# Operand addresses, residual loads and early sums in a three-layer transformer kernel on one core

## The chip, the core and the metric

The kernel runs on one core of a Trainium2 chip (trn2). The metric is the time of the whole program on the device, in microseconds; the median of three runs is compared. All data are float32; matrix products run on pairs of "fp32r" tiles: each operand is split into a high part, which ScalarE writes (`hi`), and the remainder, which VectorE writes (`lo`), and a product is three matmuls, high by high, high by low and low by high.

## The reference

Three residual layers over 1,024 rows of 1,024 columns, then a feed-forward block:

```python
# layer 0: h = rms_norm(x); proj = h @ w_in (18 feature tiles of 128)
#   sliding-window attention (8 heads) * silu(gate), pooling * silu(gate), @ w_out, rms_norm, + x
# layer 1: h = rms_norm(x); a, b, gate = h @ w_in (24 tiles)
#   depthwise causal convolution, 31 taps, of a * sigmoid(b); layer norm; silu * silu(gate); @ w_out ...
# layer 2: 16 meta rows ahead of x; proj = rms_norm(h) @ w_in (24 tiles)
#   attention with decay over all earlier rows, short convolution, head norms, @ w_out, + h
hn = rms_norm_2(h, norm_mlp_g[layer])
a = jnp.square(jax.nn.relu(jnp.einsum('bld,df->blf', hn, w_ff1[layer])))   # 1024 -> 4096
h = h + jnp.einsum('blf,fd->bld', a, w_ff2[layer])                         # 4096 -> 1024
h = rms_norm_2(h, final_norm_g)
return h[:, N_META:]
```

## The kernel before

**Products.** `project_chunk` (line 394) makes one feature tile of 128 for one chunk of rows: 8 steps of 128 inputs times 3 matmuls, 24 products, into a bank of tag `pj`. In layers 0 and 1 there are two chunks of 512 columns (`c0`, `c1`), in layer 2 three of 400, 256 and 384. The stationary operand is a weight tile; `weights` (line 375) loads it into tag `wf` of the pool `stream` and splits it into `wh` and `wl` of the same pool, two buffers each. `out_project` (line 479) makes the three out-projections, with the split rows `yh`, `yl` as stationary and the weights `wo` as moving operand, 48 products of 512 columns a row tile.

**Memory.** SBUF is filled from both ends by pools. From below: 16,384 bytes a partition that the program keeps for dynamic DMA, four constants of 32 bytes, the pool `const` (768 bytes), `stream` (six tiles of 4,096), `small` (2,432), then the pools of the stages; from above the pool `edge` and the stages' "right" pools. Tiles are rounded to 32 bytes. A pool opened over a closed one waits, tile by tile, for the last readers of what lay there.

**Order.** A planner sets the order of each engine's queue by priority (the order of the code) and its own estimate of when an instruction is ready; on the chip every queue runs in that order. All loads and stores but the gates' go through SP's queue.

**Out-projection of layer 2 and the step to the feed-forward.** `mix_ff` (line 1488) runs over eight row tiles: load `x2`, 48 products, add (`finish`, line 1536), store to `x3`, mean square, scale (`scaled`). Both feed-forward matrices are multiplied by a scheme of seven block products instead of eight (Winograd's form of Strassen's). Its right-hand operands are seven blocks of the normed rows, transposed: `b11`, `b21`, `b22` are put in the loop; `t1` to `t4` are sums of rows `i` and `i + 4`, made in `sums` (line 1546), and put behind the loop. A put (line 1526) is four transposes into a bank of tag `ps` (two buffers), `hi` on ScalarE, `lo` on VectorE. `xn7`, the scaled last row, and `gpre`, the gain, lie in the stream tag `wl`.

**First matrix.** `Up` (line 174) runs over 16 blocks `q` of the feed-forward's features: `load` (two loads of 512 KB), `top` (splits `a11`, `a12`), `sums` (four sums on GpSimd into two stream tiles `wl`, then the splits `s21`, `s34`, `a22`), and three groups of products: `first` (24), `middle` (36), `last` (24). `pair` (line 185) takes even blocks' tiles from `stream` and odd ones' from the pool `upa`. `first(0)` and `first(1)` stand in `mix_ff` behind the loop, the rest in `rest` (line 293).

**Second matrix.** `feed_down` (line 1617) makes seven steps, each over eight parts `p` of 256 features: load `act` (512 KB, tag `wf`), load or sum the weights (`w`, or the kept `x` and `y`), split both, 24 products into four banks. At each step's end the banks are added to `res`, the residual, which eight loads bring in at step 0, `p` = 1. After steps 5 and 6 `final_norm` (line 1723) squares both halves of a row tile, takes the root, scales and stores.

Of the kernel before, what the change touches and what calls it, by code (L numbers as in the profile page):

```python
# [173 lines left out]
class Up:  # L174
# [6 lines left out]
    def __init__(self, kern, hb, four):  # L181
        self.k, self.nc, self.hb, self.four = kern, kern.nc, hb, four
        self.raws, self.blocks, self.state = {}, {}, {}
# [24 lines left out]
    def sums(self, q):  # L208
        (a11, a12), (a21, a22) = ((t[:, 0:4], t[:, 4:8]) for t in self.raws.pop(q))
# [7 lines left out]
        for tag, names, src in (("s21", ("s2", "s1"), s21), ("s34", ("s3", "s4"), s34), ("a22", ("a22",), a22)):  # L217
            h, l = (self.pool.tile([128, len(names) * 4, 128], F32R, tag=tag + x, name=tag + x) for x in "hl")
# [74 lines left out]
    def rest(self):  # L293
        for q in range(self.N):
            if q > 1:
                self.first(q)
            if q:
                self.last(q - 1)
            if 0 < q < self.N - 1:
                self.load(q + 1)  # L300
                self.top(q + 1)
            self.sums(q)
            self.middle(q)
        self.last(self.N - 1)
        self.k.close(self.g, self.xp)


class Kernel:
    def __init__(self, ctx, tc, a, out):
# [5 lines left out]
        edge.tile([128, 8], F32, name="edge")  # L315
# [185 lines left out]
    def run(self):  # L501
# [3 lines left out]
        self.const.tile([128, 8], F32, name="even")  # L505
# [65 lines left out]
        ong = op[1].tile([128, 16], F32, name="ong")[:, :KD]  # L571
# [21 lines left out]
        hb, up, hp = self.mix_ff(mixed, wo, wp, early[1])  # L593
# [5 lines left out]
    def mix_out(self, layer, y, xsrc, xdst, wsrc, gpost, gpre, eps, cuts, meta, hooks={}, res=None, wo=None, soon=1, wp=None):  # L599
# [26 lines left out]
        if layer == 1:  # L626
            wq = self.pool("wq1", "right")
            wq[1].tile([128, 32], F32, name="pad")
            extra = [self.pool("e1", "right"), wq]
# [198 lines left out]
    def project_first(self, pool, chunks, jobs, holds):  # L828
# [3 lines left out]
        gain = pool.tile([128, 16], F32, name="gain", bufs=1)[:, :KD]  # L832
# [196 lines left out]
    def layer0_pooling(self, chunks, y, ahead):  # L1029
# [3 lines left out]
        psc = pool.tile([128, 16], F32, name="psc", bufs=1)[:, :4]  # L1033
# [452 lines left out]
    def mix_ff(self, y, wo, wp, four):  # L1486
# [11 lines left out]
        up = Up(self, hb, four)  # L1498
        rp = self.pool("res", "right")
# [6 lines left out]
        gpr = self.stream.tile([128, D], F32, tag="wl", name="gpre")  # L1506
# [19 lines left out]
        def put(name, i, src):  # L1526
            bank = self.ps().rearrange("p (k c) -> p k c", k=4)
# [47 lines left out]
        for t in range(1, NT):  # L1575
# [17 lines left out]
        hb.update({n: block(hp1[1], n) for n in names})  # L1593
        own = self.pool("upa")
        up.own = own[1]
        u = scaled(NT - 1, self.stream.tile([128, D], F32, tag="wl", name="xn7"))
# [18 lines left out]
        return hb, up, (own, hp1, hp0)  # L1615

    def feed_down(self, one):
# [71 lines left out]
        )  # L1689
        for n, (name, right, t0, h) in enumerate(steps):  # L1690
# [7 lines left out]
            for p in range(8):  # L1698
# [6 lines left out]
                if n == 0 and p == 1:  # L1705
                    for i in range(NT):
                        nc.sync.dma_start(out=res[:, i, :], in_=self.x3[i * 128:(i + 1) * 128, :])
                if not end:
                    for k in range(2):
                        for i in range(4):  # L1710
                            matmuls(banks[i], i, k, *ops[p], p + k == 0, p == 7 and k == 1, fresh)
            for i in range(4):
# [6 lines left out]
                if n > 4:  # L1719
                    self.final_norm(t0 + i, [res[:, t0 + i, z] for z in HALF], gfin, left[1])  # L1720
        self.close(res_pool, hold, left, xp)

    def final_norm(self, t, parts, gain, pool):
        nc = self.nc
        ms = self.tiny(2, "fms")
        for i, x in enumerate(parts):
            nc.scalar.activation(
                out=self.pj(), in_=x, func=AF.Square, scale=1.0 / 32, accum_out=ms[:, i:i + 1]
            )
        rs = self.tiny(1, "frs")  # L1730
        nc.gpsimd.tensor_tensor(out=rs, in0=ms[:, 0:1], in1=ms[:, 1:2], op=ALU.add)
        self.rsqrt(rs, rs, EPS_B)
# [79 lines left out]
```

## Time and profile before

| | us |
|---|---|
| median of 3 runs | 2005.93 (2004.78 to 2006.83) |
| the profiled execution | 1999.52 |
| its span, first to last instruction | 1997.7 |

| engine | busy us | share of the span |
|---|---|---|
| PE (TensorE) | 1924.1 | 96% |
| PEld (its weight loads) | 1619.3 | 81% |
| DVE (VectorE) | 1346.7 | 67% |
| ACT (ScalarE) | 907.5 | 45% |
| POOL (GpSimd) | 543.6 | 27% |

The stages, in us from the start: layer 0 to about 376, layer 1 to 777, layer 2's attention to 1,240, its out-projection to 1,339, the first feed-forward matrix to 1,668, the second to 1,990. The profile is one execution; its time stands beside the median for that reason. "PEclk" is the granted TensorE clock as a share of full speed. The chain of waits follows the work that ended last back from the end, at each step to what released it; pieces of one kind are merged. In lists in order of time, brackets give the engine's idle time before an instruction and what ended it. Matmuls are pipelined: one lasts some 390 ns while the next starts after some 230, so the pace is read from a piece of the chain, its length over its count.

### The profile page before, as it was taken

To read this page: it belongs to the slowest core of one execution; us is meant where nothing else is said; L and a number is where in the kernel's file an instruction comes from. 1 tells how busy PE (TensorE), PEld (TensorE's weight loads), DVE (VectorE), ACT (ScalarE), POOL (GpSimd) and SP (SyncE) were. 2 spreads that over 40 slices of the span, in tenths; PEclk is the share of its full clock that TensorE was granted. 3 is DMA by queue.
4 is the path that set the end of the run, shared out by engine and by line. 5 is a ranking of instruction groups with operands and counts; after the bars stand their busy time and mean duration, and the time that the engine had idled before them with its cause. 6 is when DMAs were issued, how large, how long until landed. Compare 5 with 4: busy or idle time off the path is not lost.

```text
span 1997.7 us, 25550 instructions
## 1 busy us (share of the span) xinstructions
PE 1924.1 (96%) x9584; PEld 1619.3 (81%) x9584; DVE 1346.7 (67%) x2045; ACT 907.5 (45%) x1577; POOL 543.6 (27%) x433
## 2 busy tenths in 40 slices
PE   7999999899999899899999999998999998899998
PEld 6888778688778678798999998886888886788886
DVE  7888656799887665565656555556767665754656
ACT  5555334455663665554444544224333333333334
POOL 4122602489996221001010101113323220000003
PEclk9999999999999899999999999998999999999999
DMA  4111144111122731111111203422444357622564
GB/s 149 59 38 33 59 136 126 36 44 53 42 69 102 231 107 55 44 44 44 48 48 46 77 22 131 148 106 78 152 161 157 137 175 294 247 98 102 183 215 150
DMA packets 121596, 212.15 MB, mean 106 GB/s; under 512 B 9449, under 2 KB 58985, under 8 KB 121473
## 3 DMA queue, kind: packets, MB, share of 16 engines
q1 hardware_dynamic: 119168, 206.34, 30.6%
q10 hardware_dynamic: 2304, 4.20, 0.6%
q8 instruction: 75, 1.23, 0.3%
q14 instruction: 49, 0.39, 0.1%
HBM read 156.46 MB, written 54.03 MB: 105 GB/s over the span
## 4 chain that ended last, share of the span: by engine, by line
PE 78%; DVE 8%; DMA 4%; POOL 4%; ACT 2%; issue 2%; SPq 0%; DVEq 0%; POOLq 0%; ACTq 0%
PE pj L400 25%; PE pd L485 11%; PE pd L227 9%; PE pd L1679 7%; PE ps L227 4%; POOL side L1129 4%; DVE acc L1135 3%; PE ps L1679 3%; PE pj L1679 3%; PE o L1410 3%; PE pj L227 2%; PE ps L1386 2%; PE pt L1435 2%; DVE wl L361 1%; DMA y<-in_ff 1%
## 5 line engine op out<-in xcount | busy, mean ns | idle before, releaser
L1129 POOL TENSOR_TENSOR side<-side,tap 128x1024 f32<-128x1024 f32 (+1 forms) x99 | 236.1, 2392 | 20.5 <-ACT tap L1128 13.4
L1135 DVE SCALAR_TENSOR_TENSOR acc<-glu,dw,acc 128x1024 f32<-128x1024 f32 (+1 forms) x162 | 193.8, 1238 | 11.5 <-ACT acc L1133 10.3
L400 PE MATMUL pj<-c0h,wl 128*128 128x512 f32 (+1 forms) x496 | 189.3, 382 | 7.0 <-DVE wl L361 7.0
L400 PE MATMUL pj<-c0h,wh 128*128 128x512 f32 (+1 forms) x496 | 190.4, 384 | 2.2 <-ACT gt L1166 2.1
L400 PE MATMUL pj<-c0l,wh 128*128 128x512 f32 (+1 forms) x496 | 189.0, 381 | 0.0
L400 PE MATMUL pj<-c1h,wh 128*128 128x512 f32 (+1 forms) x496 | 176.7, 357 | 3.3 <-ACT c1h L357 1.6
L400 PE MATMUL pj<-c1h,wl 128*128 128x512 f32 (+1 forms) x496 | 176.8, 356 | 0.0
L400 PE MATMUL pj<-c1l,wh 128*128 128x512 f32 (+1 forms) x496 | 176.7, 356 | 0.0
L1128 ACT ACTIVATE tap<-glu,dw 128x1024 f32<-128x1024 f32 (+1 forms) x99 | 103.7, 1054 | 78.1 <-POOL side L1129 77.5
L357 ACT ACTIVATE ah<-act 128x1024 fp32r<-128x1024 f32 x56 | 59.3, 1061 | 160.8 <-PE ps L1679 74.4
L361 DVE TENSOR_TENSOR al<-act,ah 128x1024 fp32r<-128x1024 f32 x56 | 68.2, 1223 | 91.5 <-ACT ah L357 91.5
L357 ACT ACTIVATE ph<-pt 128x512 fp32r<-128x512 f32 (+3 forms) x144 | 72.5, 516 | 101.1 <-PE pt L1435 66.4
L361 DVE TENSOR_TENSOR wl<-wf,wh 128x1024 fp32r<-128x1024 f32 (+1 forms) x66 | 95.4, 1445 | 25.1 <-ACT wh L357 22.9
L1679 PE MATMUL pd<-bh,ah 128*128 128x512 f32 x256 | 100.3, 397 | 12.4 <-ACT ah L357 12.4
L400 PEld LDWEIGHTS pj<-c0h,wl 128*128 128x128 f32 x496 | 94.4, 190 | 21.6 <-DVE wl L361 7.5
L400 PEld LDWEIGHTS pj<-c1h,wh 128*128 128x128 f32 x496 | 93.4, 188 | 18.7 <-ACT c1h L357 1.8
L400 PEld LDWEIGHTS pj<-c0h,wh 128*128 128x128 f32 x496 | 94.3, 190 | 16.9 <-ACT gt L1166 2.5
L361 DVE TENSOR_TENSOR pl<-pt,ph 128x512 fp32r<-128x512 f32 (+3 forms) x144 | 82.9, 586 | 36.8 <-ACT ph L357 36.2
L400 PEld LDWEIGHTS pj<-c0l,wh 128*128 128x128 f32 x496 | 94.3, 190 | 14.2 <-issue 0.2
L400 PEld LDWEIGHTS pj<-c1l,wh 128*128 128x128 f32 x496 | 93.4, 188 | 14.0 <-DVE c1l L361 0.4
L400 PEld LDWEIGHTS pj<-c1h,wl 128*128 128x128 f32 x496 | 93.5, 188 | 13.3
L1679 PE MATMUL pd<-bl,ah 128*128 128x512 f32 x256 | 100.9, 394 | 0.0
(600 smaller groups left out, 5120.1 us busy)
## 6 DMA issues: line engine op xcount, KB each, us to landing
wf<-in_w SPq DMA_DIRECT2D x63, 512.0 KB, 3.5
raw<-in_ff SPq DMA_DIRECT2D x32, 512.0 KB, 4.9
w<-in_ff SPq DMA_DIRECT2D x32, 512.0 KB, 4.4
act<-acts SPq DMA_DIRECT2D x32, 512.0 KB, 3.2
acts<-s SPq DMA_DIRECT2D x48, 256.0 KB, 3.8
act<-act SPq DMA_DIRECT2D x24, 512.0 KB, 3.8
wf<-in_wo SPq DMA_DIRECT2D x20, 512.0 KB, 3.8
cb<-cum SPq DMA_DIRECT2D x8, 520.0 KB, 4.1
```

Source lines behind the costliest of these rows:

```text
L227: self.nc.tensor.matmul(out=bank, lhsT=st[:, k, :], rhs=mv[:, k, :], start=(start and k == 0 and j == 0), stop=(k == 3 and j == 2), skip_g ...
L357: self.nc.scalar.activation(out=out, in_=src, func=AF.Copy, scale=scale)
L361: return self.nc.vector.tensor_tensor(out=out, in0=src, in1=hi.bitcast(F32), op=ALU.subtract)
L400: self.nc.tensor.matmul(out=p[:m, :n], lhsT=st[:, k, :], rhs=mv[:, k, :], start=(k == 0 and j == 0), stop=(k == KD - 1 and j == 2),)
L485: self.nc.tensor.matmul(out=ops[hf], lhsT=st, rhs=mv[:, HALF[hf]], start=(first and k == ks[0] and j == 0), stop=(last and k == ks[-1] and ...
L1128: nc.scalar.activation(out=tap, in_=src, func=AF.Copy, scale=w)
L1129: nc.gpsimd.tensor_tensor(out=side, in0=side, in1=tap, op=ALU.add)
L1135: nc.vector.scalar_tensor_tensor(out=acc, in0=src, scalar=w, in1=acc, op0=ALU.mult, op1=ALU.add)
L1386: nc.tensor.matmul(out=s[:, :b0 - a0], lhsT=q[e][:, n * 128:(n + 1) * 128], rhs=k[e][j][:, a0:b0], start=(j == 0), stop=(j == 1),)
L1410: nc.tensor.matmul(out=ov[:, cols], lhsT=v[e][:rows, j, :], rhs=mv, start=first, stop=(last and jj == 1),)
L1435: nc.tensor.transpose(pt[:, c:c + 128], ts[i][:, META + 128 * j:META + 128 * (j + 1)], self.ident)
L1679: nc.tensor.matmul(out=bank, lhsT=st[:, k, c], rhs=mv[:, k, :], start=(fresh and first and j == 0), stop=(last and j == 2), skip_group_che ...
```

## The change

1. The program is told to keep 2,048 bytes a partition for dynamic DMA instead of 16,384.
2. `Even`, a wrapper around every pool that `Kernel.pool` opens, rounds tiles up to multiples of 64 elements (256 bytes). Fill tiles are added to or enlarged in `edge`, `const`, `small` and `wq1`.
3. `gpre` moves from `stream` into the pool of `res`, `xn7` into the place of `t4`'s low half. `Up.sums` is cut in two: `add_up` (the GpSimd sums) and `split_sums`. For block 0, `add_up` and the split of `s21` (into a new pool `up21`) are written at the end of the out-projection's loop, the splits of `s34` and `a22` behind the puts. The puts behind the loop are regrouped name by name around `first(0)`, `load(1)`, `top(1)` and `first(1)`; `t2` and `t3` go through banks of tag `pj`.
4. In `feed_down`, `res` is loaded in four quarters of four row tiles by half the columns, each at `p` = 3 of the step that first adds to it.
5. In step 6 the half of each row that is complete is squared, and the epsilon added, ahead of the last products.

```diff
+    def add_up(self, q):
         (a11, a12), (a21, a22) = ((t[:, 0:4], t[:, 4:8]) for t in self.raws.pop(q))
...
+        self.wide[q] = {"s21": (("s2", "s1"), s21), "s34": (("s3", "s4"), s34), "a22": (("a22",), a22)}
+
+    def split_sums(self, q, tags):
+        for tag in tags:
+            names, src = self.wide[q].pop(tag)
+            pool = self.early if tag == "s21" else self.pool
+            h, l = (pool.tile([128, len(names) * 4, 128], F32R, tag=tag + x, name=tag + x) for x in "hl")
             self.split(h, l, src)
...
-            self.sums(q)
+            if q:
+                self.sums(q)
...
+class Even:
+    def tile(self, shape, dtype, **kw):
+        n = int(np.prod(shape[1:]))
+        if n % 64 == 0:
+            return self.pool.tile(shape, dtype, **kw)
+        t = self.pool.tile([shape[0], n + -n % 64], dtype, **kw)[:, :n]
+        return t if len(shape) == 2 else t.rearrange("p (a b) -> p a b", b=shape[2])
...
-        edge.tile([128, 8], F32, name="edge")
+        edge.tile([128, 56], F32, name="edge")
+        self.const.tile([128, 32], F32, name="even")
...
-        return g, g.__enter__()
+        return g, Even(g.__enter__())
...
-        self.const.tile([128, 8], F32, name="even")
+        self.const.tile([128, 8], F32, name="even2")
+        self.small.tile([128, 8], F32, tag="even3", name="even3")
...
+        ep = self.pool("up21", "right")
+        up.early = ep[1]
         rp = self.pool("res", "right")
...
-        gpr = self.stream.tile([128, D], F32, tag="wl", name="gpre")
+        gpr = rp[1].tile([128, D], F32, name="gpre")
...
+        up.add_up(0)
+        up.split_sums(0, ("s21",))
         self.close(tp, wp)
         hp1 = self.pool("h3b")
...
-        for n in names[:2]:
-            for i in range(3):
-                put(n, i, rows[i][n])
-        up.load(1)
-        sums(3, u)
-        for n in names[:2]:
-            put(n, 3, rows[3][n])
+        banks = {"t2": self.pj, "t1": self.ps, "t3": self.pj, "t4": self.ps}
+        def all_puts(n):
+            for i in range(4):
+                put(n, i, rows[i][n], banks[n])
+        sums(3, scaled(NT - 1, xn7[:, 0:2].rearrange("p a b -> p (a b)")))
         self.close(*xp[::-1])
         up.xp = self.psum_pool("pxup", "pd")
         up.first(0)
+        all_puts("t2")
+        up.load(1)
+        all_puts("t1")
         up.top(1)
-        for n in names[2:]:
-            for i in range(4):
-                put(n, i, rows[i][n])
+        all_puts("t3")
         up.first(1)
+        hb["t4"] = block(hp1[1], "t4")
+        all_puts("t4")
         self.close(rp)
         up.g = self.pool("up", "right")
         up.pool = up.g[1]
+        up.split_sums(0, ("s34", "a22"))
...
+        quarters = {0: (0, 0), 1: (4, 1), 2: (0, 1), 4: (4, 0)}
...
-                if n == 0 and p == 1:
-                    for i in range(NT):
-                        nc.sync.dma_start(out=res[:, i, :], in_=self.x3[i * 128:(i + 1) * 128, :])
+                if p == 3 and n in quarters:
+                    r0, c = quarters[n]
+                    for i in range(r0, r0 + 4):
+                        nc.sync.dma_start(out=res[:, i, HALF[c]], in_=self.x3[i * 128:(i + 1) * 128, HALF[c]])
...
+            if n == 6:
+                for i in range(4):
+                    ms = squares[i] = self.tiny(2, "fms")
+                    junk = left[1].tile([128, 512], F32, tag="r", name="junk")
+                    self.half_square(ms, 1, res[:, t0 + i, HALF[1]], junk)
+                    nc.gpsimd.tensor_scalar(
+                        out=ms[:, 1:2], in0=ms[:, 1:2], scalar1=EPS_B, scalar2=None, op0=ALU.add
+                    )
...
-    nc = bacc.Bacc("TRN2", target_bir_lowering=False, num_devices=1)
+    nc = bacc.Bacc("TRN2", target_bir_lowering=False, num_devices=1, dynamic_dma_scratch_size=2048)
```

## Rows read from the trace of the kernel before

**Rows 1.** Busy by stretch: length; PE, PEld, DVE, ACT, POOL; PEclk, DMA share, GB/s

```profile
37.00:260.00 223.00, 220.87 (x1142) 185.65 (x1142) 179.21 (x393) 109.05 (x260) 65.87 (x58) 1.00 0.14 47
...
390.00:570.00 180.00, 170.15 (x722) 136.82 (x722) 170.54 (x152) 106.79 (x112) 163.28 (x69) 0.98 0.14 47
570.00:651.00 81.00, 80.27 (x340) 64.50 (x340) 63.22 (x55) 41.58 (x47) 62.49 (x28) 0.98 0.28 96
...
1339.00:1372.00 33.00, 24.79 (x123) 18.98 (x122) 24.63 (x33) 15.38 (x25) 6.89 (x6) 0.88 0.23 80
...
1667.00:1729.00 62.00, 49.06 (x198) 38.73 (x197) 37.21 (x34) 21.51 (x22) 0.00 (x0) 0.94 0.96 365
```

**Rows 2.** The chain of waits, whole span: start, length, what, merged count

```profile
333.09 28.44 PE pd L485 x124
...
600.53 33.46 PE pj L400 x144
...
777.23 4.37 PE pj L400 x24
...
1435.73 2.77 PE pj L227 x12
...
1454.82 2.72 PE pj L227 x12
...
1772.36 43.52 PE pd L1679 x192
```

**Rows 3.** TensorE in order of time, layer 1's gates: start, length, what, idle before

```profile
570.62 0.50 PE L400 MATMUL pj<-c0h,wh 128*128 128x512 f32 x1 [2.08 <-ACT gt L1166]
```

**Rows 4.** Groups by line and shape, TensorE: count | busy us, mean ns | idle

```profile
L400 PE MATMUL pj<-c0h,wh 128*128 128x400 f32 x184 | 64.6, 351 | 0.0
...
L400 PE MATMUL pj<-c0h,wv 128*128 128x400 f32 x16 | 4.4, 348 | 0.7 <-DVE q L363 0.7
```

**Rows 5.** TensorE in order of time, out-projection to feed-forward

```profile
1338.93 1.03 PE L1529 MATMUL ps<-ident,res 128*128 128x128 f32 x8
...
1360.51 1.96 PE L1529 MATMUL ps<-ident,res 128*128 128x128 f32 x8 [0.81 <-DVE t2l L361]
1363.03 1.11 PE L1529 MATMUL ps<-ident,res 128*128 128x128 f32 x4 [0.56 <-DVE t3l L361]
...
1371.22 0.79 PE L227 MATMUL pd<-t2h,s21h 128*128 128x512 f32 x1 [1.63 <-ACT s21h L357]
```

**Rows 6.** VectorE and GpSimd in order of time, the same stretch

```profile
1342.73 1.29 DVE L1521 SCALAR_TENSOR_TENSOR xn<-res,rs,gpre 128x1024 f32<-128x1024 f32 x1
...
1346.40 2.28 DVE L361 TENSOR_TENSOR a<-raw,a 128x1024 fp32r<-128x1024 f32 x1
...
1355.00 1.28 DVE L361 TENSOR_TENSOR t1l<-ps,t1h 128x512 fp32r<-128x512 f32 x2
...
1365.08 1.27 POOL L216 TENSOR_TENSOR sums<-raw 128x512 f32<-128x512 f32 x1 [17.49 <-PE ps L1529]
```

**Rows 7.** VectorE in order of time, the first reader of `gpre`

```profile
1268.21 1.28 DVE L1521 SCALAR_TENSOR_TENSOR xn<-res,rs,gpre 128x1024 f32<-128x1024 f32 x1 [1.50 <-POOL rs L430]
```

**Rows 8.** SP's queue and TensorE in order of time, start of the second matrix

```profile
1691.77 9.59 SPq L1707 DMA_DIRECT2D res<-x3s  x8
...
1716.84 0.50 PE L1679 MATMUL pd<-bh,ah 128*128 128x512 f32 x1 [3.17 <-ACT ah L357]
```

**Rows 9.** All engines in order of time, the end of the span

```profile
1991.43 0.58 ACT L1727 ACTIVATE pj<-res 128x512 f32<-128x512 f32 x1
...
1992.49 0.22 POOL L427 TENSOR_SCALAR frs<-frs 128x1 f32<-128x1 f32 x1
```

**Rows 10.** DMA queues (packets, MB, share); issues: count, KB, median us to landing

```profile
q1 hardware_dynamic: 119168, 206.34, 30.6%
...
w<-in_ff SPq DMA_DIRECT2D x32, 512.0 KB, 4.4
...
act<-acts SPq DMA_DIRECT2D x32, 512.0 KB, 3.2
```

More of the change, by code (lines that the diff above doesn't have):

```diff
@@ L182, in __init__ @@
         self.k, self.nc, self.hb, self.four = kern, kern.nc, hb, four
-        self.raws, self.blocks, self.state = {}, {}, {}
+        self.raws, self.blocks, self.state, self.wide = {}, {}, {}, {}
     def pair(self, q, tag):
@@ L208, in sums @@
     def sums(self, q):
+        self.add_up(q)
+        self.split_sums(q, ("s21", "s34", "a22"))
+    def add_up(self, q):
         (a11, a12), (a21, a22) = ((t[:, 0:4], t[:, 4:8]) for t in self.raws.pop(q))
@@ L570, in run @@
         wo, stage = {}, {}
-        ong = op[1].tile([128, 16], F32, name="ong")[:, :KD]
+        ong = op[1].tile([128, KD], F32, name="ong")
         nc.sync.dma_start(out=ong, in_=a["ong"])
@@ L592, in run @@
         wp = self.layer2(chunks, last, fs, early, ahead, prefetch)
-        hb, up, hp = self.mix_ff(mixed, wo, wp, early[1])
+        up, hp = self.mix_ff(mixed, wo, wp, early[1])
         up.rest()
@@ L831, in project_first @@
         nc.vector.memset(ones, 1.0)
-        gain = pool.tile([128, 16], F32, name="gain", bufs=1)[:, :KD]
+        gain = pool.tile([128, KD], F32, name="gain", bufs=1)
         ws = [
@@ L1032, in layer0_pooling @@
         pool = pb[1]
-        psc = pool.tile([128, 16], F32, name="psc", bufs=1)[:, :4]
+        psc = pool.tile([128, 4], F32, name="psc", bufs=1)
         nc.sync.dma_start(out=psc, in_=a["psc"])
@@ L1524, in scaled, with put @@
             return out
-        def put(name, i, src):
-            bank = self.ps().rearrange("p (k c) -> p k c", k=4)
+        def put(name, i, src, bank=self.ps):
+            bank = bank().rearrange("p (k c) -> p k c", k=4)
             for k in range(4):
@@ L1592, in mix_ff @@
         names = ("t2", "t1", "t3", "t4")
-        hb.update({n: block(hp1[1], n) for n in names})
+        hb.update({n: block(hp1[1], n) for n in names[:3]})
+        xn7 = hp1[1].tile([128, 4, 512], F32, tag="t4l", name="xn7")
         own = self.pool("upa")
         up.own = own[1]
-        u = scaled(NT - 1, self.stream.tile([128, D], F32, tag="wl", name="xn7"))
-        for n in names[:2]:
-            for i in range(3):
-                put(n, i, rows[i][n])
-        up.load(1)
-        sums(3, u)
-        for n in names[:2]:
-            put(n, 3, rows[3][n])
+        banks = {"t2": self.pj, "t1": self.ps, "t3": self.pj, "t4": self.ps}
[3 more added lines that the diff above has]
+        sums(3, scaled(NT - 1, xn7[:, 0:2].rearrange("p a b -> p (a b)")))
         self.close(*xp[::-1])
@@ L1614, in mix_ff @@
         up.pool = up.g[1]
-        return hb, up, (own, hp1, hp0)
+        up.split_sums(0, ("s34", "a22"))
+        return up, (ep, own, hp1, hp0)
     def feed_down(self, one):
@@ L1719, in feed_down, with half_square, final_norm @@
                 if n > 4:
-                    self.final_norm(t0 + i, [res[:, t0 + i, z] for z in HALF], gfin, left[1])
+                    self.final_norm(t0 + i, [res[:, t0 + i, z] for z in HALF], gfin, left[1], squares.get(i))
         self.close(res_pool, hold, left, xp)
-    def final_norm(self, t, parts, gain, pool):
+    def half_square(self, ms, i, x, junk):
+        self.nc.scalar.activation(out=junk, in_=x, func=AF.Square, scale=1.0 / 32, accum_out=ms[:, i:i + 1])
+    def final_norm(self, t, parts, gain, pool, ms=None):
         nc = self.nc
[L1725 to L1729, printed above, removed]
+        before = ms is not None
+        if not before:
+            ms = self.tiny(2, "fms")
+            self.half_square(ms, 1, parts[1], self.pj())
+        self.half_square(ms, 0, parts[0], self.pj())
         rs = self.tiny(1, "frs")
         nc.gpsimd.tensor_tensor(out=rs, in0=ms[:, 0:1], in1=ms[:, 1:2], op=ALU.add)
-        self.rsqrt(rs, rs, EPS_B)
+        self.rsqrt(rs, rs, 0.0 if before else EPS_B)
         for h, x in zip(HALF, parts):
```

7 lines of the change are left out of this document (4 added, 3 removed).

## The prediction

> **What bounds the kernel now.** I read the busy times by stretch first, to see which engine fills which stage; then the chain of waits for the pace of TensorE inside them; then the order of time wherever TensorE stood idle. TensorE fills layer 0 (220.87 of 223 us) and the gates of layer 1 (80.27 of 81); it has holes in the convolution (170.15 of 180), between the out-projection and the feed-forward (24.79 of 33, at a granted clock of 0.88) and where the second feed-forward matrix begins (49.06 of 62, with the DMA engines 0.96 busy) [rows 1]. So two things are worth having: less time per product where TensorE is full, and the holes where it waits.
>
> The pace is read from pieces of the chain that hold products alone: length over count. Layer 1's products take 33.46/144 = 232.4 ns, layer 0's out-projection 28.44/124 = 229.4, the second feed-forward matrix 43.52/192 = 226.7, all for 512 columns [rows 2]. Within one line the same difference is seen: `product` with the streamed weights of an even block takes 2.77 us for twelve, with those of an odd block 2.72 [rows 2]. Both have the same shape and the same moving operand `b21`. What differs is where the weights lie: `pair` puts even blocks into the stream pool and odd ones into the pool `upa`. The stream pool begins at 16,384 + 128 (constants) + 768 (the const pool) = 17,280 bytes, 67.5 times 256; `upa` follows 24,576 bytes of stream and 2,432 of small tiles at 44,288, which is 173 times 256, plus whole tiles of 4,096. So the slow rows are those whose stationary operand starts half a step off a multiple of 256.
>
> **Part 1, addresses.** I work the new plan out by hand: 2,048 + 128 + 896 = 3,072 for stream, 27,648 for small, 30,208 for the first pool, and 229,120 for the top of the right side; every pool between is rounded by `Even`. All weights and all moving tiles then start on multiples of 256, but for slices inside the 400-column chunk. Gains, each times its count:
> - Layer 0: 15 feature tiles x 2 chunks x 24 products = 720, at 232.4 - 226.7 = 5.7 ns: 4.1 us. TensorE is full there.
> - Layer 1: 1,152 products, but only the some 340 after 570 us count [rows 1]: there TensorE stood 2.08 us until ScalarE had emptied a gate bank [rows 3], and ScalarE was in its queue behind taps that GpSimd's sums hold up. That instant doesn't move with TensorE. 340 x 5.7 = 1.9 us; the other 812 give 0 while the convolution is later (4.6 if it isn't).
> - Out-projections: 1,152 x (229.4 - 226.7 = 2.7) = 3.1 us.
> - Feed-forward, even blocks: 192 x (2.77 - 2.72)/12 = 0.8 us.
> - Layer 2's narrow products, some 1,560: no stretch of the trace shows the pair cleanly. 182.1 ns is the pace of a misplaced 400-column product (4.37/24) [rows 2]; with aligned weights (`wv`) 400 columns last 348 ns, with the stream's 351 [rows 4]. Bounds are 0 and the 5.7 of the wide ones (8.9 us); I take 1 ns, 1.6 us, nearer to the row of the same width.
>
> Sum 11.5 us, bounds 7 and 20. The Trainium skill's page "SBUF — State Buffer" (section "Operand start alignment") asks only that an operand start at a multiple of its element size, says that this is "about legality, not speed", and names no 256; its section on the DMA port swizzle gives lines of 16 bytes, on which the old addresses begin too. By that rule this part is worth 0. The two paces of `product` [rows 2] speak against it, and no run here has yet moved an address alone.
>
> **Part 2, between out-projection and feed-forward.** The out-projection's products end at 1,338.9, where transposes follow, and the first product of `middle(0)` starts at 1,371.2 [rows 5]. Between them lie 18 puts of four transposes (eight take 1.03 us [rows 5], so some 0.5 each, 9.0) and the 48 products of `first(0)` and `first(1)` (48 x 0.2267 = 10.9): 19.9 us of work in 32.3. The puts set the pace: two banks, and each waits for ScalarE's and then VectorE's half, so a pair takes 1,363.03 - 1,360.51 = 2.52 us [rows 5]. Last comes a wait of 1.63 us for `s21h` [rows 5]; GpSimd made one of its sums only at 1,365.08, after 17.49 us without work, when the stream buffer that the last row was in had been read [rows 6].
> After the change `s21` is summed and split inside the loop. Added there are four GpSimd sums (1.27 each), 1.05 us of ScalarE and 1.23 of VectorE, beside the loop's products, which keep TensorE busy while VectorE has holes. A VectorE subtraction beside a GpSimd sum took 2.28 us [rows 6] where its like takes 1.23, so up to 4 us of VectorE may come on top; if that cover were gone, TensorE would lose the same 4. The two stream buffers are free, since `gpre` and `xn7` move out. `gpre` now waits for the attention's space, but its first reader stands at 1,268.21 [rows 7], behind the first row's whole out-projection. `load(1)` moves behind the puts of `t2`; on SP's queue it is still behind the last store of `x3`, and nothing there waits on it. Its data go to `top(1)` and then to `first(1)`, which now stands behind three sets of puts.
> The puts get four banks instead of two, and `first(0)` covers the chain to the last row: scaled at 1,342.73 + 1.29, then three subtractions of 0.69, to about 1,346.1 [rows 6]. From 1,344 VectorE bounds: 18 halves at 0.64 (two take 1.28 [rows 6]), four evacuations and two subtractions at 0.69 and a split of 1.23 are 16.9 us, so the puts end near 1,361; TensorE's own work would end at 1,338.9 + 19.9 = 1,358.8. I take 1,361 for `middle(0)`: 10 us. The stretch lost 33 x (1 - 0.88) = 4 us of clock [rows 1], most of it under waits; I count 1.5 for the products in it. Together 11.5; bounds 5 (the pair's pace stays) and 14 (no hole at all). Late next is `s34`, which still waits until the last put has read `res`; two groups of twelve products (5.4 us) cover its 2.3.
>
> **Part 3, `res` in quarters.** Before, eight loads of 512 KB took SP's queue from 1,691.77 for 9.59 us, and TensorE stood 3.17 us until 1,716.84 for an `act` tile issued behind them [rows 8]. The three earlier waits there stand ahead of `res` and belong to `x`, `y` and `act`. Bounds: 0, because the quarters have no earlier reader to wait for and the planner can issue all sixteen as soon as the space is free, in the same 0.96 busy stretch; 5, if the last wait goes with its clock. I take 2, nearer to nothing.
>
> **Part 4, the tail.** One square (0.58 us, with its reading some 0.6) and one addition on GpSimd (0.22, with the hand-over some 0.3) leave the last row's chain [rows 9]: 0.9 us. The four early squares lie beside the last step's products, where ScalarE is free.
>
> Sum: 11.5 + 11.5 + 2 + 0.9 = 26. The profiled execution took 1,999.52 us (span 1,997.7), 6.4 below the median of 2,005.93; I take the difference from the median: 1,980.
>
> **Rivals.**
> - The address has no effect, and the two paces of `product` have another cause that the stream pool keeps, say that ScalarE and VectorE write its buffers while they are read: 2,005.9 - 14.4 = 1,991.5. For it: the 400-column rows differ by 1% only [rows 4]. Against: `upa` is written in the same way, and the paces differ within one line. Chance 0.10. The page's rule above would end here.
> - Part 2 gives 3 us instead of 11.5: the puts keep their place in TensorE's in-order queue in front of products that are ready, and VectorE's halves still set the pace. For it: VectorE is busy for most of that stretch (24.63 of 33 us [rows 1]). 1,989. Chance 0.20.
> - More than forecast: the convolution gives its 4.6, narrow products 4 more, the last wait of part 3 goes: 1,968. Chance 0.12.
> - Slower: the smaller scratch. If the transfer queue (206.34 MB through one queue of the kind "hardware_dynamic" [rows 10]) keeps its descriptors in those 16,384 bytes, 2,048 hold an eighth, and loads no longer overlap. The place is the second feed-forward matrix: a step of 24 products (24 x 226.7 = 5.4 us) needs an `act` and a `w` load, which land in 3.2 and 4.4 us [rows 10], 7.6 in series: 2.2 us x 32 = 70 us, to 2,050. It decides once two loads can't be in flight together. Against: no row shows a queue whose descriptors an engine writes. Chance 0.05. By the skill's same page (section "SBUF size: 192, 224, or 256?") the scratch serves only transfers whose descriptors GpSimd writes; no queue of the trace is called that.
> - The gains are eaten by a new order of the queues, the whole being planned anew: about 2,004. Chance 0.05.
>
> **How the numbers follow.** Forecast 1,980 with chance 0.48. The likeliest case's own bounds are some 1,973 to 1,989; the range takes in the first three rivals, 1,967 to 1,994, and leaves out the last two and the ends of the unknown costs. A measurement of this kernel tells 0.2%, 4 us, from no change. Faster 0.90, within 0.2% 0.05, slower 0.05.
>
> **What would show it.** Part 1: chain pieces of layers 0 and 1 at 227 ns a product, both parities of `product` at 2.72. Part 2: from the last out-projection product to `middle(0)` some 22 us instead of 32, without a wait for `s21h`. Part 3: no wait of 3 us near the start of the second matrix's last loads. Part 4: one square between the last addition and the scale. Wrong if the pace stays at 232, if the puts still come in pairs of 2.5 us, or if a stage elsewhere has a wait that it hadn't.

## The result and the profile after

The changed kernel takes 1,977.09 us (median of four, 1,975.94 to 1,978.88), the kernel before 2,005.36 beside it: ratio 0.986, 95% interval 0.984 to 0.988. That is 28 us less; 26 less and 1,980 were forecast. The profiled executions differ by 23.5 us of span (1,997.7 to 1,974.2): the profiled one of before, 1,999.52 us, is the shortest of that kernel, whose others shown here took 2,002 to 2,012.

Busy times by stretch of the kernel after answer [rows 1] (length; PE, PEld, DVE, ACT, POOL; PEclk, DMA share, GB/s): layer 0, the convolution, the gates, the step to the feed-forward from the out-projection's end, the start of the second matrix.

```profile
37.00:260.00 223.00, 220.14 (x1141) 186.44 (x1142) 178.67 (x392) 109.71 (x262) 66.57 (x58) 0.99 0.15 49
390.00:570.00 180.00, 168.97 (x726) 138.16 (x727) 169.81 (x152) 106.93 (x112) 163.41 (x68) 0.98 0.14 49
570.00:651.00 81.00, 79.02 (x351) 64.47 (x350) 61.87 (x53) 42.74 (x50) 60.18 (x28) 0.99 0.31 102
...
1328.00:1361.00 33.00, 30.97 (x166) 25.21 (x165) 25.53 (x35) 16.23 (x28) 7.54 (x6) 1.00 0.21 74
...
1643.00:1705.00 62.00, 49.45 (x198) 38.90 (x198) 38.14 (x35) 22.21 (x23) 0.00 (x0) 0.94 0.96 365
```

The step is mended: 166 products and transposes in 33 us at a clock of 1.00 instead of 123 at 0.88. The start of the second matrix isn't: 198 products in 62 us, as before, the DMA engines at 0.96 again.

For the rest of the reading I cut the trace of each kernel at the same products. Each number is the difference of two row times, in us of span:

| stage | before | scratch alone | + addresses | + parts 3, 4 | after (+ part 2) |
|---|---|---|---|---|---|
| layers 0 and 1, to the last product of 1's out-projection | 776.7 | 777.7 | 773.2 | 772.0 | 772.0 |
| layer 2's attention, to its first out-projection product | 460.2 | 454.5 | 453.3 | 453.2 | 453.4 |
| its out-projection | 102.3 | 102.3 | 102.1 | 102.1 | 102.1 |
| step and first matrix | 328.7 | 327.2 | 328.8 | 328.4 | 316.1 |
| second matrix with the wait ahead of it | 322.1 | 324.0 | 323.7 | 323.7 | 321.9 |
| tail, after the last product | 7.8 | 7.8 | 7.8 | 8.6 | 8.6 |
| span | 1997.7 | 1993.5 | 1988.8 | 1988.1 | 1974.2 |
| median | 2005.4 | 1996.5 | 1991.1 | 1992.4 | 1977.1 |

The parts are numbered as in the prediction; the middle columns are the first experiments.

How far do single traces differ by stage where nothing was changed? Nine of the kernels measured here (those with part 1's addresses and `shift_128`) run the same instructions in the same order in layers 0 and 1, and took 772.0 to 776.2 us there, 773.7 on average; the three without those addresses took 776.7 to 778.9, 777.8 on average. From the first product of the second matrix to the last the changed kernel took 318.5 us, and `tail_pair`, which differs only in its last products, 321.2. So 3 to 4 us in one of these stages between two single traces prove nothing.

### The profile page after: what moved, and what is told of

Same layout as the page of the kernel before. It is cut to its first block, busy times and chain, and to the rows that moved or that the text cites. A ratio compares the mean times of both kernels' runs of the same rounds, so it can differ in the third digit from the quotient of the medians.

```text
span 1974.2 us, 25561 instructions
## 1 busy us (share of the span) xinstructions
PE 1906.5 (97%) x9584; PEld 1616.1 (82%) x9584; DVE 1340.4 (68%) x2045; ACT 906.0 (46%) x1577; POOL 542.5 (27%) x433
## 5 line engine op out<-in xcount | busy, mean ns | idle before, releaser
L1161 DVE SCALAR_TENSOR_TENSOR acc<-glu,dw,acc 128x1024 f32<-128x1024 f32 (+1 forms) x162 | 193.8, 1238 | 11.5 <-ACT acc L1159 10.2
L425 PEld LDWEIGHTS pj<-c0h,wh 128*128 128x128 f32 x496 | 94.1, 190 | 18.4 <-ACT gt L1192 3.1
L386 DVE TENSOR_TENSOR wl<-wf,wh 128x1024 fp32r<-128x1024 f32 (+1 forms) x66 | 90.6, 1373 | 23.5 <-ACT wh L382 23.2
```

The source lines that it names most:

```text
L386: return self.nc.vector.tensor_tensor(out=out, in0=src, in1=hi.bitcast(F32), op=ALU.subtract)
L425: self.nc.tensor.matmul(out=p[:m, :n], lhsT=st[:, k, :], rhs=mv[:, k, :], start=(k == 0 and j == 0), stop=(k == KD - 1 and j == 2),)
L1161: nc.vector.scalar_tensor_tensor(out=acc, in0=src, scalar=w, in1=acc, op0=ALU.mult, op1=ALU.add)
```

## The experiments

### The parts, one on top of the other

`scratch_only` is the kernel before with one argument more (shown here), `addr_only` has `Even` and the fill tiles too, `no_step` also parts 3 and 4 (the `res` quarters and the tail).

```diff
-    nc = bacc.Bacc("TRN2", target_bir_lowering=False, num_devices=1)
+    nc = bacc.Bacc("TRN2", target_bir_lowering=False, num_devices=1, dynamic_dma_scratch_size=2048)
```

> The kernel before with 2,048 instead of 16,384 bytes kept for dynamic transfers, and nothing else. All pools from below move by 14,336 bytes, 56 times 256, so every start keeps its place within 256. Theory: the scratch does nothing here, 2,005 within 4 us, pace 232, transfers land in the same 3.2 to 4.4 us. Rival (transfers throttled): some 2,050, landings of `act` and `w` longer. Rival (it is the room that counts, and the address is an accompaniment): faster by several us with 232 ns kept.

> The kernel before with the addresses alone: the smaller scratch, `Even` and the fill tiles; `gpre`, `xn7`, the puts, `res` and the tail as before. Address theory: the wide products of layers 0 and 1 go from 232 to 227 ns, the out-projections from 231 to 228, and the time falls by 11.5 us (7 to 20), to about 1,994, ratio 0.994; layer 1's first 812 products give nothing, since the convolution ends last. Rival (the address does nothing, the stream pool is slow for another cause): 232 ns stays, 2,005. The trace of the changed kernel gained some 5 us between 790 and 900 us that no step of mine named: if the new addresses (or the planning that they bring) did it, it shows here too and the time is nearer to 1,990; if the early sums' planning did it, it doesn't.

> The changed kernel without its second part: `gpre`, `xn7`, the sums of block 0, the puts and the loads of block 1 as before; addresses, `res` quarters and tail as changed. Theory: the stretch between the last product of the out-projection and the first of `middle(0)` goes back from some 15 to 32 us of span with 8 us of holes, and a wait for `s21h` of 1.6 us returns; 10.4 us slower than the changed kernel, about 1,987.5. Rival (the puts' pace stays VectorE's): 3 us, 1,980.

Measured against before: 0.9947 (0.9927 to 0.9967), 0.9919 (0.9903 to 0.9936) and 0.9932 (0.9911 to 0.9952). So the smaller scratch alone is worth 9.6 us by the medians, 4.2 in the profiled executions, where I had put nothing; the addresses add 5 (5.4 and 4.7) where I had 11.5; parts 3 and 4 add nothing; part 2 gives the rest, 15.3 and 13.9, where I had 11.5.

What the scratch moved shows in layer 2's attention: the first 130 us of it, before, then with the scratch alone.

```profile
777.00:907.00 130.00, 121.03 (x759) 109.75 (x758) 83.73 (x210) 70.34 (x154) 11.49 (x10) 0.97 0.15 48
```

```profile
777.70:907.70 130.00, 125.22 (x795) 115.71 (x793) 83.23 (x221) 74.38 (x166) 11.51 (x10) 0.97 0.15 48
```

TensorE gets 36 more products into the same time, at the same granted clock. In order of time, TensorE's longest wait of that stretch is this one before:

```profile
819.60 0.70 PE L1386 MATMUL ps<-kh,q 128*128 128x400 f32 x1 [3.68 <-DVE mn L1393]
```

and this one with the scratch alone, about as long; but before, waits of 1.03, 0.71 and 1.61 us (at 801.6, 811.3 and 900.1) come on top, of which the scratch alone leaves one of 0.56:

```profile
813.11 0.67 PE L400 MATMUL pj<-c0h,wv 128*128 128x400 f32 x1 [3.36 <-DVE q L363]
```

The products stand in another order in the queue, and `addr_only` has that order too. That leaves two causes for the gain: the order, or the transfers.

### The scratch without its room

```diff
-        self.const = ctx.enter_context(tc.tile_pool(name="const", bufs=1))
+        self.const = ctx.enter_context(tc.tile_pool(name="const", bufs=1)); ctx.enter_context(tc.tile_pool(name="room", bufs=1)).tile([128, 3584], F32, name="room")
...
-    nc = bacc.Bacc("TRN2", target_bir_lowering=False, num_devices=1)
+    nc = bacc.Bacc("TRN2", target_bir_lowering=False, num_devices=1, dynamic_dma_scratch_size=2048)
```

> The kernel before with 2,048 bytes kept for dynamic transfers and a fill tile of the 14,336 bytes set free: every pool lies where it lay before, and every engine's queue holds the same instructions in the same order as before; the kernel with the smaller scratch alone had another order (its product of `kh` and `q` at 819 us, and those about it). Theory (the smaller scratch gave its 9.6 us through the room, which lets the planner choose another order): 2,005 within 4 us, no gain. Rival (the size of the scratch itself makes transfers cheaper): 1,996.

2,006.06 us, ratio 0.9995 (0.9984 to 1.0006). The fill tile stands behind `const`, so that pool alone lies 14,336 bytes lower. In its trace every queue has the order of the kernel before, and layer 2's attention takes 460.5 us again. The size of the scratch does nothing that these runs could tell; the gain of `scratch_only` came with where the pools lie, and with the order that the planner then chose (no run changed one of these without the other). The slower rival of the prediction (2,050) falls here too.

### The start of the operands

`shift_128` resizes two fill tiles, so that every pool lies 128 bytes off; `left_128`, further down, resizes only `even`, the one at the lower end.

```diff
-        self.const.tile([128, 32], F32, name="even")
+        self.const.tile([128, 64], F32, name="even")
-        edge.tile([128, 56], F32, name="edge")          # shift_128 only
+        edge.tile([128, 24], F32, name="edge")
```

> The changed kernel with two fill tiles resized, so that every pool of SBUF starts 128 bytes past a multiple of 256; all else is kept. Address theory: the 512-column products go back to 232 ns in layers 0 and 1 and, since now every operand is off, in the second matrix too, where the kernel before had 226.7: 720 + 340 + 1,152 + some 1,150 products of the first matrix + 700 of the second at 5.5 ns, 15 to 20 us slower than the changed kernel, about 1,994. If only the stationary operand counts the same. Rival (address without effect): 1,977, pace 227.

1,980.74 us, 0.9868 (0.9852 to 0.9884): the pace didn't go back. TensorE in the two feed-forward matrices, 200 us each, of the changed kernel and of `shift_128`:

```profile
1400.00:1600.00 200.00, 200.00 (x885) 165.64 (x884) 138.22 (x149) 70.34 (x97) 63.91 (x44) 1.00 0.45 154
1750.00:1950.00 200.00, 200.00 (x884) 165.68 (x883) 118.00 (x112) 80.82 (x97) 13.86 (x16) 1.00 0.48 163
```

```profile
1400.00:1600.00 200.00, 200.00 (x884) 165.60 (x883) 138.91 (x150) 70.02 (x96) 65.73 (x44) 1.00 0.44 151
1750.00:1950.00 200.00, 200.00 (x884) 165.62 (x883) 121.26 (x116) 77.78 (x90) 13.04 (x12) 1.00 0.49 163
```

884 products in 200 us are 226 ns each, with not one operand on a multiple of 256 bytes. My rule was wrong, though its number wasn't. So I measured the cost by itself (none of the reference is computed):

> The disputed cost by itself: none of the reference is computed. Blocks of 96 fp32r products, each with a new stationary tile (eight take turns), stationary operands that start 0, 64, 128 or 192 bytes past a multiple of 256 (tiles sa to sd) against moving operands with the same four starts (ma to md), all sixteen pairs at 512 columns, once in one order and once in the reverse; 400 and 256 columns with 0 and 128. The run with everything 128 bytes off kept 226.7 ns, so the first theory (each operand must start on a multiple of 256) is down. Theory now: what counts is that both starts are alike modulo 256. It gives 226.7 ns on the four pairs of equal starts, 22 us a block, and 232 on those that differ by 128; those that differ by 64 lie between or at 232. Rival (the pace depends on what writes into the same memory at the time, not on the starts): 226.7 everywhere, since nothing is written here. At 400 and 256 columns no difference over 1 ns by either.

TensorE in order of time: start, length, moving and stationary tile (a, b, c, d start 0, 64, 128, 192 bytes past a multiple of 256), columns, count.

```profile
54.45 22.15 PE L34 MATMUL o<-mb,sa 128*128 128x512 f32 x96
76.44 22.48 PE L34 MATMUL o<-mc,sa 128*128 128x512 f32 x96
98.76 22.55 PE L34 MATMUL o<-md,sa 128*128 128x512 f32 x96
121.15 22.56 PE L34 MATMUL o<-ma,sb 128*128 128x512 f32 x96
143.55 21.94 PE L34 MATMUL o<-mb,sb 128*128 128x512 f32 x96
165.33 22.15 PE L34 MATMUL o<-mc,sb 128*128 128x512 f32 x96
...
386.61 17.44 PE L34 MATMUL o<-ma,sa 128*128 128x400 f32 x96
403.89 17.76 PE L34 MATMUL o<-ma,sc 128*128 128x400 f32 x96
421.49 17.76 PE L34 MATMUL o<-mc,sa 128*128 128x400 f32 x96
...
456.37 11.67 PE L34 MATMUL o<-ma,sa 128*128 128x256 f32 x96
467.88 11.56 PE L34 MATMUL o<-ma,sc 128*128 128x256 f32 x96
479.28 11.55 PE L34 MATMUL o<-mc,sa 128*128 128x256 f32 x96
```

From start to start over 96, at 512 columns: equal starts (`mb`,`sb`) 226.9 ns; moving 64 past stationary (`mb`,`sa`; `mc`,`sb`) 229.1; 128 past 232.5; 192 past (`md`,`sa`; `ma`,`sb`) 233.2 and 233.3. All sixteen pairs fall on these four values, in both orders: only the difference of the two starts modulo 256 counts, as far as these four starts show. At 400 columns 128 bytes cost 3.3 ns (180.0 to 183.3), at 256 nothing (119.9 to 118.8). Nothing wrote into the operands' tiles meanwhile (VectorE copied one bank a block into another tile), so that rival is down too. The Trainium skill's page "SBUF — State Buffer" (section "Operand start alignment") says of its rule that it "is about legality, not speed"; it doesn't deny this cost, it is silent on it.

> The changed kernel with one fill tile resized, so that the pools of the left side (the streamed weights among them) start 128 bytes past a multiple of 256 and those of the right side on one; all else is kept. Theory (starts must be alike): products of a streamed weight with an operand of the right side go to 232 ns, in layers 0 and 1 above all (some 1,730 of them seen at one clock), and the time rises by 4 to 10 us over the changed kernel's 1,977, nearer to 4, since the addresses alone gave 4.7 us of span between two kernels of the same scratch. Rival (starts have no part in it): 227 ns stays, and the time is within 3 us of the changed kernel's.

2,003.79 us, 0.999 (0.998 to 1.000): all of the change's gain is gone, far more than the 4 to 10 us expected. The two matrices:

```profile
1400.00:1600.00 200.00, 200.00 (x861) 161.44 (x861) 136.18 (x146) 69.52 (x96) 63.94 (x43) 1.00 0.45 154
1750.00:1950.00 200.00, 200.00 (x862) 162.18 (x861) 109.95 (x101) 71.82 (x72) 0.00 (x0) 1.00 0.43 144
```

232 ns each. The expectation named the wrong stages: in layers 0 and 1 the moving chunks lie on the left side as well and kept 227.5, while both matrices, most of whose products now pair the two sides, lost 16 us together. Another 9 us went in layer 2's attention (462.0 us against 453.4); its order of products differs from the changed kernel's, and the waits there are those of before again. So that stage's gain hangs on an order that 128 bytes can tip. The last 5 us (777.0 against 772.0) lie in layers 0 and 1, hardly more than traces differ there without a cause.

### The step: banks

```diff
-        banks = {"t2": self.pj, "t1": self.ps, "t3": self.pj, "t4": self.ps}
+        banks = dict.fromkeys(names, self.ps)
```

> The changed kernel with all sixteen puts behind the loop through the two banks of tag ps, as in the kernel before, instead of ps and pj in turn; the early s21 and the new order of the puts around `first(0)` and `first(1)` stay. The step from out-projection to feed-forward holds 1.8 us of holes in the changed kernel (1.20 and 0.59) and 8.2 in the one before. Theory (the early sums and the products placed between the puts close the holes, the banks add little): within 2 us of the changed kernel, 1,977 to 1,979. Rival (four banks are what breaks the pairs of 2.5 us): 3 to 6 us of holes return at the puts, 1,980 to 1,983.

1,984.39 us, 0.9884 (0.9865 to 0.9902), 7.3 us slower than the changed kernel: my theory fell. TensorE at the last puts of `two_banks`:

```profile
1357.10 1.25 PE L1557 MATMUL ps<-ident,res 128*128 128x128 f32 x8 [1.03 <-DVE t1l L386]
1359.17 1.04 PE L1557 MATMUL ps<-ident,res 128*128 128x128 f32 x4 [0.82 <-DVE t3l L386]
...
1361.63 1.60 PE L1557 MATMUL ps<-ident,res 128*128 128x128 f32 x8 [0.56 <-DVE t3l L386]
1364.15 1.26 PE L1557 MATMUL ps<-ident,res 128*128 128x128 f32 x8 [0.93 <-DVE t4l L386]
1366.22 0.80 PE L236 MATMUL ps<-t1h,s21h 128*128 128x512 f32 x1 [0.81 <-DVE t4l L386]
```

The pairs of 2.5 us are back, without a wait for `s21h`. The step with the first matrix takes 323.2 us instead of 316.1, so 7 of the 12 us of part 2 hang on the banks; the early sums alone don't close the holes. Idle time makes up only half of the 7: TensorE's waits in that stage sum to 5.3 us instead of 2.0. The rest fits the clock, which fell around these holes, where the changed kernel's row above has 1.00; 0.06 of 37 us are 2.2:

```profile
1330.00:1367.00 37.00, 31.67 (x161) 25.13 (x160) 25.09 (x33) 15.79 (x27) 4.82 (x4) 0.94 0.17 57
```

The planner also moved products: 48 of the first matrix have started 13.5 us after the out-projection's last product, instead of 18.4. So the 7 us are the price of two banks with the order that they bring. How the other 5 divide between the early sums and the regrouped puts, no run shows.

### `res`, `x` and `y` held back

The changed kernel's quarters, and then those of `res_held`, on SP's queue:

```profile
1668.44 14.45 SPq L1743 DMA_DIRECT2D res<-x3s  x16
```

```profile
1668.39 3.90 SPq L1744 DMA_DIRECT2D res<-x3s  x4
...
1703.66 1.74 SPq L1744 DMA_DIRECT2D res<-x3s  x4
...
1745.64 1.74 SPq L1744 DMA_DIRECT2D res<-x3s  x4
```

As written, all sixteen loads leave together as soon as there is room, and hold the queue for 14.45 us where eight took 9.59 [rows 8]. One copy of four columns makes each quarter wait:

```diff
                     r0, c = quarters[n]
+                    nc.vector.tensor_copy(out=res[:, r0:r0 + 4, 512 * c], in_=t[:, 0, 0:4])
```

> The changed kernel, where one small copy of VectorE into each quarter of `res` (columns of the part that has just landed, overwritten by the load) makes the quarter's loads wait for that part; in the changed kernel all sixteen loads left together, 14.45 us on the queue of SyncE. Theory (the loads of `res` are what the last waits at the start of the second matrix stand behind): the waits of 3.9 and 2.7 us shrink, 2.5 to 5 us faster than the changed kernel, 1,972 to 1,975. Rival (those waits belong to the other loads there, which fill the DMA engines anyway): within 1 us of 1,977.

1,972.77 us, 0.9837 (0.9822 to 0.9852), 4.3 us less than the changed kernel; in the traces the second matrix is 2.6 us shorter (319.3 against 321.9). TensorE's waits at the start of the second matrix, changed kernel, then `res_held`:

```profile
1647.14 0.73 PE L1713 MATMUL pd<-bh,ah 128*128 128x512 f32 x1 [3.48 <-ACT ah L382]
1662.03 0.50 PE L1713 MATMUL pd<-bh,ah 128*128 128x512 f32 x1 [2.09 <-ACT ah L382]
1677.09 0.50 PE L1713 MATMUL pd<-bh,ah 128*128 128x512 f32 x1 [3.89 <-ACT ah L382]
1692.58 0.50 PE L1713 MATMUL pd<-bh,ah 128*128 128x512 f32 x1 [2.68 <-ACT ah L382]
```

```profile
1647.08 0.50 PE L1713 MATMUL pd<-bh,ah 128*128 128x512 f32 x1 [3.43 <-ACT ah L382]
1662.83 0.50 PE L1713 MATMUL pd<-bh,ah 128*128 128x512 f32 x1 [2.98 <-ACT ah L382]
1678.19 0.61 PE L1713 MATMUL pd<-bh,ah 128*128 128x512 f32 x1 [4.16 <-ACT ah L382]
```

The last wait is gone, the other three stay: those belong to other loads. `y_tail` and `xy_tail` hold these back in the same way (with `res` held, and the tail of the next section):

```diff
...
+                if n == 0 and p < 6:                                   # xy_tail only
+                    x = kept["x", p + 2] = tile("x", p + 2)
+                    nc.scalar.copy(out=x[:, 0, 0:4], in_=t[:, 0, 0:4])
+                    weights(0, 0, p + 2, x, nc.scalar)
+                if n == 1:
+                    y = kept["y", p] = tile("y", p)
+                    nc.scalar.copy(out=y[:, 0, 0:4], in_=t[:, 0, 0:4])
+                    weights(1, 1, p, y, nc.scalar)
...
```

> The changed kernel with `res` held back by quarters, the last two row tiles taking turns, and `y` held back too: each of its eight loads is issued on ScalarE's queue in step 1, behind a small copy from the `act` tile of the same part, instead of all eight at the start of step 0. Theory (the waits at the second matrix's start come from loads that are issued long before they are wanted): of the waits that stayed with `res` held, 3.4, 3.0 and 4.2 us, the second and the third shrink by 2 to 5 us together; with 0.9 of the tail the time falls from 1,972.8 to 1,967 to 1,970. Rival (`act` and `w` come late by themselves, whatever else moves): the waits stay, 1,972.

> The same with `x` held back as well: two of its eight loads as before, the other six two parts ahead of their use, on ScalarE's queue behind a copy from the `act` tile of the current part. Theory: `act` of the first parts no longer stands behind 4 MB of `x`; 1 to 3 us less again, 1,965 to 1,968. Rival (a chain of `act`, copy, load and split is now longer than a part's products of 5.4 us, so `x` itself comes late): a new wait in each of the parts 2 to 7, 1 to 2 us each, 6 us slower than with `y` alone.

1,969.48 us, 0.982 (0.9803 to 0.9838), and 1,964.91, 0.9801 (0.9786 to 0.9816). With `y` held the waits are 3.65 and 2.09; with `x` too one is left:

```profile
1648.78 0.75 PE L1713 MATMUL pd<-bh,ah 128*128 128x512 f32 x1 [3.66 <-ACT ah L382]
```

The second matrix with the wait ahead of it takes 310.2 us instead of 321.9. This version is 12 us faster than the changed kernel, and 41 faster than the one before.

### The tail

TensorE's last product, then VectorE, ScalarE and GpSimd behind it, of the changed kernel:

```profile
1965.22 0.39 PE L1713 MATMUL pd<-bh,al 128*128 128x512 f32 x1
...
1966.07 1.41 DVE L1784 SCALAR_TENSOR_TENSOR out<-res,frs,gfin 128x512 f32<-128x512 f32 x2 [1.09 <-POOL frs L455]
1967.41 0.68 DVE L1763 TENSOR_TENSOR res<-res,pd 128x512 f32<-128x512 f32 x1
1968.18 0.60 ACT L1769 ACTIVATE pj<-res 128x512 f32<-128x512 f32 x1 [3.04 <-DVE res L1763]
...
1969.83 1.41 DVE L1784 SCALAR_TENSOR_TENSOR out<-res,frs,gfin 128x512 f32<-128x512 f32 x2 [1.75 <-POOL frs L455]
```

From the last addition to the scale are 2.42 us; before it was 3.40 (from 1,990.00 to 1,993.40, around [rows 9]). The early square saves its 0.98. But the addition starts 1.80 us after the last product, behind the scale of the row tile before; in the kernel before the change it started at once. `tail_pair` lets the last two row tiles' products take turns, so that both additions come first:

```diff
...
+                if n == 6 and i != 3:
+                    for p, r in ((6, (i,)), (7, (i,))) if i < 2 else ((6, (2, 3)), (7, (2, 3))):
+                        for q in r:
...
```

> The changed kernel, where the last step's products of its last two row tiles take turns, so that both are ready about together. Theory (the tail didn't shorten because VectorE's queue has the scale of the last row but one ahead of the last addition, 1.8 us after the last product): the last addition starts within 0.3 us of the last product, the tail from the last product's end to the end of the span falls from 8.55 to some 6.8 us, the time by 1.7, to 1,975.4; a difference that only the trace can show. Rival (the early squares themselves cost the tail): it stays at 8.5.

The median is 1,980.03 (0.9868, 0.9851 to 0.9886), which can't tell 1.7 us. In the trace the addition starts at 1,971.26, 0.04 after the last product's end. So the theory of the queue holds for that wait, but the tail is 7.7 us, not 6.8: GpSimd's two small steps now run beside VectorE's scale and take 0.37 and 0.94 us, where they took 0.19 and 0.55.

## Why the prediction was right, point by point

The time was right, partly by errors that cancel. Made from the median, the sum gave 1,980 for 1,977.09; from the profiled execution it gives 1,973.5 for the profiled 1,975.94.

**Part 1, 11.5 us forecast; 4.7 of span (5.4 by the medians) measured for the addresses, and 4.2 to 9.6 beside them.** That is below the lower bound too. The bounds, 7 and 20, don't follow from the part's own rows: those add up to 9.9 without the narrow products, and to 23.4 with the upper ends. The pace improved as said: the chain's piece of layer 1's gates goes from 33.46 us for 144 products [rows 2] to this, in `xy_tail`, the one kernel whose chain has it without a wait:

```profile
598.23 32.74 PE pj L425 x144
```

227.4 ns instead of 232.4. In `addr_only` the same piece takes 33.40 us: the products follow each other at 227.7 ns there too, but pauses of up to 0.1 us stand between single ones. In the changed kernel `product` takes 2.72 us for even and odd blocks alike. Three steps failed. The rule was the wrong one: not a multiple of 256, but equal starts modulo 256 (`phases`, `shift_128`); the two paces of `product` [rows 2] had shown a pair with a difference of 128 and a pair without, and I read it off the stationary operand alone. Second, the gain of layers 0 and 1 (4.1, 1.9 and, of their out-projections, 2.1: 8.1) came out at 4.5 in this pair of traces (4.1 by the averages above). The convolution took what it was forecast to take: from `scratch_only` to `addr_only` TensorE's waits between 460 and 600 us grew by 0.7, 1.7, 0.6, 0.7 and 0.3 while the products shrank. In layer 0 the 720 products fell from 232.3 to 228.0 ns, 3.1 us, but the first product of the out-projection starts only 0.7 us earlier: the wait at some 241 us grew from 0.84 to 1.53, and the granted clock from 220 to 250 us was 0.94 instead of 1.00, some 1.8 us more (behind that wait some products follow each other at 427 ns, the lower of the clock's two levels). So "TensorE is full there" was the step that was wrong. Third, layer 2's attention gave 1.3 where 1.6 was forecast for its narrow products, which is luck: 256 and 400 columns gain nothing, 384 gain 1.4 ns (175.7 to 174.3). Of the other terms, the third out-projection gave 0.1 of its 1.0, and the 0.8 of the even blocks is in no stage: step and first matrix took 1.6 longer. And I gave the smaller scratch two outcomes, nothing or slower. It had a third, which stands only among the rivals of `scratch_only`: the room that it frees lets the planner choose another order. That is the "new order of the queues" of my last rival, with the other sign. The Trainium skill's page "SBUF — State Buffer" (section "SBUF size: 192, 224, or 256?") calls this reserve a ring buffer for SWDGE descriptors, which by the page's terms GpSimd writes. `scratch_fill` agrees, with its ratio of 0.9995 where the trace names no such queue.

**Part 2, 11.5 forecast; 12.3 in its own stages, 13.9 of span, 15.3 by the medians.** TensorE between the out-projection's end and the first product of `middle(0)`, changed kernel:

```profile
1327.37 0.60 PE L1557 MATMUL ps<-ident,res 128*128 128x128 f32 x4
...
1340.10 0.73 PE L236 MATMUL pd<-b11h,a 128*128 128x512 f32 x2 [1.20 <-DVE a L386]
...
1345.53 0.48 PE L236 MATMUL pd<-t2h,s21h 128*128 128x512 f32 x1
...
1351.41 0.50 PE L236 MATMUL pj<-b21h,a 128*128 128x512 f32 x1 [0.59 <-DVE t3l L386]
```

18.2 us instead of 32.3, with no wait for `s21h`; 22 were forecast. Of the 18 puts that stood ahead of that product, 11 still do, so the like-for-like gain is the stage's 12.3, not these 14. Holes of 1.8 us are left of 8.2. The clock's 1.5 us were named, and the row shows 1.00. `two_banks` shows that the four banks, which the working named as one cause among several, carry 7 us of it, with the order that they bring.

**Part 3, 2 forecast; 0 as far as the traces tell.** From the first product of the second matrix to the last, `addr_only` (whole loads) takes 320.29 us and `no_step` (quarters) 320.32; waits of 3.89 and 2.68 us still stand in the changed kernel, where the sign of success was none of 3. The lower bound's reason was the right one, and I didn't take it: the loads leave together. `res_held` shows that most of the upper bound, 5, was to be had (4.3 by the medians).

**Part 4, 0.9 forecast; 0.8 lost.** The term was right (0.98), but the step left out the queue: a shorter chain made the row before ready earlier, and the planner put its scale ahead of the last addition. Like the longer waits of the convolution, this is a wait that wasn't there before, one of the prediction's own signs of being wrong.

Of the rivals, "no effect of the address" falls with `phases` and `left_128`, "part 2 gives 3 us" with `no_step`, "slower" with `scratch_fill`.

Two things stay open. The profiled execution of before lies some 6 us below that kernel's median, and of the 9.6 us of the scratch 5 are in no trace. Against the trace of `scratch_fill`, which has the same instructions in the same order and spans 2,001.7 us, the gain is 8.2, so most of the 5 may be this one short execution. And `shift_128`, whose queues hold the changed kernel's instructions in the same order, is 3.6 us slower by medians whose intervals overlap; 3.8 us of span lie in its second matrix, where the DMA engines are full. `tail_pair`, which differs from the changed kernel only in its last products, has 2.6 us of the same there, so no cause in the addresses is needed.

## What to carry to other kernels

A tile written earlier in the code isn't loaded later: a planner issues a load as soon as its space is free, so a load that should wait needs something to wait for, and a four-column copy from the tile that it should follow is enough. When an edit makes one chain shorter, look at what then stands ahead of it in the next in-order queue. And undo a change in parts before its sum is believed: here a sum right to 3 us held one term twice too large, and the runs hold a gain that nobody had forecast.

## What the runs showed of the hardware

An fp32r product of 512 columns takes 226.9 ns when stationary and moving operand start alike modulo 256 bytes, and 229.1, 232.5 or 233.2 when the moving one starts 64, 128 or 192 bytes further (`phases`); at 400 columns 128 bytes cost 3.3 ns, at 256 nothing. A multiple of 256 isn't needed, as `shift_128` shows with every operand 128 bytes off.
